# One stacked value product for half of the attention heads, their denominators on VectorE, and key blocks of two head groups in turn

## The chip, the core and the metric

The kernel runs on one core of a Trainium2 chip. The metric is the device time of one execution in microseconds (us).

## What is computed

One encoder layer over 2048 tokens of width 1024. The normalised input goes through one projection whose columns feed two head groups: a gated linear attention (GLA, 4 heads) and a softmax attention with 8 query heads on 2 key/value heads (kv = 0 and 1, four query heads each, head width 64). Both outputs are concatenated, projected, and added to the input; then a mixture of 64 experts follows (each token uses two), and a last norm. The part that changes is the softmax attention:

```
def attend(qb):
    s = jnp.einsum('bkgqd,bksd->bkgqs', qb, kh).astype(jnp.float32)
    p = jax.nn.softmax(s, axis=-1).astype(vh.dtype)
    return jnp.einsum('bkgqs,bksd->bkgqd', p, vh)
```

## The kernel before

The tokens are 16 tiles of 128. A first stage projects the input and stores q, k and v; a second computes the GLA inside chunks and the row maxima of the scores (`maxpass`); the third, which the change touches, holds attention, the output projection and the routing; the fourth runs the experts. Matmuls use a form of f32 with fewer mantissa bits (F32R), so each f32 operand is split into a high part and the low rest, and products of parts are added.

In the third stage a **group** is a token tile i and a kv, and a **key block** is a group and one of 16 tiles of 128 keys: 512 blocks, in the order of `units` (L826): all 16 blocks of a group, then the next group, tiles from the last to the first. A key block (`key_block`, L1310) computes scores of 128 keys by 4 heads x 128 queries with two matmuls into `ps` (L1328, L1329; the second adds the low parts and the negated row maximum), takes the exponential on ScalarE into `p` (L1332), casts it to its high part `p_h` (L1340; on VectorE for two of 16 key tiles, `HDVE`), subtracts to get the low rest `p_l` on VectorE (L1343), and adds three products to the group's accumulator `pa` in PSUM (L1354 to L1356). V holds per key [low (64), high (64), one, one]: high and ones by p_h, low by p_h, high and ones by p_l. The ones give the softmax denominators in rows 64 and 65 of `pa`.

After a group's last block `normalise` (L933) copies `pa` to SBUF on ScalarE (L938), which frees the accumulator (there are two), turns it with four transposes on TensorE (L943), and on VectorE takes the reciprocal of the denominator and multiplies (L949, L950). After kv = 1 of a tile `project` (L974) norms, projects with 48 matmuls (L1007), adds the residual, norms again, and routes the tile's tokens. `gla_out` (L867) finishes the tile's GLA output. The last tile has steps of its own (`linear_half`, `last_part`, `last_rows`), after which the token lists of the experts are ready and the first expert's rows are gathered. `load_ahead` (L1385), issued with the last product, starts the loads of the first expert weights.

The order of instructions on TensorE, VectorE, ScalarE and GpSimd is fixed when the program is built: `Plan` (L121) lets every step ask for an engine with an estimated duration, the tokens it depends on and buffer slots, and each time issues the step that could start first; among those that could start at once, the one whose due time less its urge is smallest. SLOT is the pace by which the due time of the next scores is set. On the chip each engine executes its list in that order and waits on semaphores. SP issues the loads, q of a group by `load_q` (L771) into two buffers.

Of the kernel before, what the change touches and what calls it, by code (L numbers as in the profile page):

```python
# [16 lines left out]
P = 128  # L17
T = 2048
NT = T // P
# [18 lines left out]
GST = 11  # L38
SLOT = 1.7
PACE = 1.6  # L40
# [21 lines left out]
PACE1 = 1.1  # L62
UE, UH, UL, UV = (1,2,3,1)
LPA = 0.2
# [132 lines left out]
def hybrid_encoder_kernel(ctx, tc, x, norm1_gain, w_in, gla_up_fwd, gla_up_fwd_bias, gla_up_bwd,  # L197
# [392 lines left out]
    with ExitStack() as ph:  # L590
# [80 lines left out]
        def maxpass(i):  # L671

            q1 = sp.tile([P, H, P], F32R, name="q1")
            nc.sync.dma_start(q1.bitcast(F32), d_q1[i])
            nm = sp.tile([P, H, 2], F32, name="nm")
            for h in range(H):
                for b in range(2):
                    pm = pp.tile([P, 2, 512], F32, name="pm", bufs=2)
                    for j in range(2):
                        c0 = (2 * b + j) * 512  # L680
                        nc.tensor.matmul(pm[:, j], lhsT=q1[:, h, :], rhs=K1[:, h // 4, c0:c0 + 512],  # L681
                                         start=True, stop=True)
                    nc.vector.tensor_reduce(nm[:, h, b:b + 1], pm, axis=AX.XY, op=OP.max, negate=True)  # L683
                    yield
            nr = sp.tile([P, H], F32R, name="nr")
            nc.vector.tensor_reduce(nr, nm, axis=AX.X, op=OP.min)
            pt = bank("pt")
            nc.tensor.transpose(pt[0:H, 0:P], nr.bitcast(F32), ident)
            nT = sp.tile([H, P], F32, name="nT")
            nc.scalar.copy(nT, pt[0:H, 0:P])  # L690
            nc.sync.dma_start(d_q2[i, DH:DH + 1].rearrange("o h t -> (o h) t"), nT)
            yield
# [87 lines left out]
        for i in range(NT):  # L780
# [3 lines left out]
            if i + 1 < NT:  # L784
                load_u(i + 1)
                decay(i + 1)
            else:

                right.close()
                kvp = right.enter_context(tc.tile_pool(name="pkv", bufs=1, side="right", reuse_waits="tile"))  # L790
                K2 = kvp.tile([DH + 1, NKV, T], F32R, name="K2")
                V = kvp.tile([P, NT, NKV, VW], F32R, name="V")
                nc.sync.dma_start(K2.bitcast(F32), d_K2)
                nc.sync.dma_start(V.bitcast(F32), d_V)
                qp = right.enter_context(tc.tile_pool(name="pcq", bufs=2, side="right", reuse_waits="tile"))
                for kv in range(NKV):
                    load_q(NT - 1, kv)
            g, m = gla(i), maxpass(NT - 1 - i)
# [11 lines left out]
    with ExitStack() as ph:  # L810
# [14 lines left out]
        order = list(reversed(range(NT)))  # L825
        units = [(i, kv, kt) for i in order for kv in range(NKV) for kt in range(NT)]  # L826
        NU, last = len(units), order[-1]
        plan = Plan({"ps": 3, "p_h": NPH, "p_l": NPL, "p": NPP, "acc": 2, "den": 2, "pt": 2, "pm": 1, "mTg": 1, "mTa": 1, "xT": 1,
                     "h": 1, "gla": 1, "route": 1, "on": 1, "oa": 1, "w": 0, "mtg": 0})
        add, give = plan.add, plan.give  # L830
        mTs, ons, acc_o = {}, {}, {}
        prev = [None, None, None, None]
# [7 lines left out]
        def rsqrt_steps(dst, ss, n, t0):  # L840

            w = ss.shape[-1]
            hx = sp.tile([P, w], F32, name=f"hx{w}", bufs=4)
            t = sp.tile([P, w], F32, name=f"nt{w}", bufs=4)
            v = nc.vector
# [87 lines left out]
        def normalise(i, kv, tv):  # L933
# [3 lines left out]
            oa = sp.tile([P, 512], F32, name="oa", bufs=1)  # L937
            nc.scalar.copy(oa[0:DH + 2], pa)  # L938
            give(t, "acc")
            t = yield ask("pe", 0.45, t, take=("on", "pt") if kv == 0 else ("pt",))  # L940
            pt = pp.tile([P, 4, P], F32, name="pt", bufs=2)
            for h in range(4):
                nc.tensor.transpose(pt[:, h, 0:DH + 2], oa[0:DH + 2, h * P:(h + 1) * P], ident[0:DH + 2, 0:DH + 2])  # L943
            give(t, "oa")
# [343 lines left out]
        def list_columns(i, o12, at, vals, *t):  # L1288
# [19 lines left out]
            return t  # L1308

        def key_block(u):  # L1310

# [4 lines left out]
            if u + 1 < NU:  # L1316
                if kt == NT - 1 and u + NT + 1 < NU:
                    load_q(*units[u + NT + 1][:2])
                    Q[units[u + NT + 1][:2]] += (landed(ts),)
                if kv == 0 and kt == GST:  # L1320
# [12 lines left out]
            give(t, "ps")  # L1333
            hd = kt in HDVE or (u < HN and kt in HD0)
            if hd:
# [7 lines left out]
            nc.vector.tensor_tensor(p_l, p, p_h.bitcast(F32), op=OP.subtract)  # L1343
            give(tl, "p")

            tv = yield ask("pe", 0.7, tl, take=(("acc", f"v{u}") if kt == 0 else (f"v{u}",)), urge=UV)
            if kt == 0:
                acc_o[i, kv] = pp.tile([P, 512], F32, name="pa", bufs=2)[0:DH + 2]
            plan.slots.pop(f"v{u}")
            plan.slots[f"v{u + 1}"] = [(0.0, "pe")]  # L1350

            pa = acc_o[i, kv]
            hi = V[:, kt, kv, DH:2 * DH + 2]
            nc.tensor.matmul(pa, lhsT=hi, rhs=p_h, start=(kt == 0), stop=False)  # L1354
            nc.tensor.matmul(pa[0:DH], lhsT=V[:, kt, kv, 0:DH], rhs=p_h, start=False, stop=False)  # L1355
            nc.tensor.matmul(pa, lhsT=hi, rhs=p_l, start=False, stop=(kt == NT - 1))  # L1356
            give(tv, "p_l", "p_h")
# [368 lines left out]
```

## Time and profile before

| | |
|---|---|
| median of 3 runs | 2979.42 us (2977.94 to 2983.98) |
| the profiled execution | 2981.33 us, of which its span 2979.4 us |
| TensorE busy | 2812.6 us (94%) |
| VectorE busy | 2225.4 us (75%) |
| ScalarE busy | 1852.0 us (62%) |

The shares are averages over four stages with different limits; the third stage lies between about 771 and 1690 us. A matmul's recorded time is longer than the distance to the next one's start, so TensorE's busy time does not tell how many matmuls could still be placed.

### The profile page before, as it was taken

How to read it: one execution, taken by the hardware profiler on the slowest of the kernel's cores; microseconds unless marked ns; L12 is line 12 of the kernel's file. 1: busy time of each engine (PE TensorE's matmuls, PEld its weight loads, DVE VectorE, ACT ScalarE, POOL GpSimd, SP SyncE). 2: the span in 40 equal slices, each digit the busy share in tenths (PEclk: the TensorE clock that was granted, in tenths of full speed). 3: DMA queues.
4: the chain of work that ended last, by engine and by line, in shares of the span. 5: the costliest groups of instructions: out<-in, count | busy, mean ns of one | idle time of the engine just before them, and what ended most of it. 6: DMA issues, size and time to landing. Idle time of an engine off the chain costs nothing.

```text
span 2979.4 us, 38648 instructions
## 1 busy us (share of the span) xinstructions
PE 2812.6 (94%) x13776; PEld 2101.0 (71%) x13776; DVE 2225.4 (75%) x3222; ACT 1852.0 (62%) x2776; POOL 448.4 (15%) x326
## 2 busy tenths in 40 slices
PE   7999899999999999999999799999999999999992
PEld 6888688887677777777776566676676666666771
DVE  6655688888676677776666788888788878778783
ACT  4433333333677777777776567777777777777773
POOL 3433111111000000000000121111111112122111
PEclk9999999999899999999999899999999999999996
DMA  7884422233521121121221799999999999999986
GB/s 254 283 279 162 149 105 91 94 105 118 198 66 63 63 80 59 61 80 58 66 77 42 249 371 365 358 355 353 352 364 353 354 353 357 350 345 357 353 311 236
DMA packets 175140, 647.00 MB, mean 217 GB/s; under 512 B 38885, under 2 KB 53575, under 8 KB 119325
## 3 DMA queue, kind: packets, MB, share of 16 engines
q1 hardware_dynamic: 136766, 590.92, 54.3%
q0 software_dynamic: 23712, 34.36, 5.3%
q10 hardware_dynamic: 14464, 19.21, 2.0%
q8 instruction: 109, 1.79, 0.2%
q14 instruction: 89, 0.73, 0.1%
HBM read 546.08 MB, written 117.13 MB: 223 GB/s over the span
## 4 chain that ended last, share of the span: by engine, by line
PE 59%; DMA 21%; issue 7%; DVE 6%; ACT 5%; POOL 1%; ACTq 0%; SPq 0%; POOLq 0%; DVEq 0%
DMA raw<-in_w_gate_dram 10%; DMA raw<-in_w_up_dram 7%; PE pm L1007 6%; PE pm L681 4%; PE pa L1356 4%; PE ps L1328 4%; PE pa L1354 4%; PE pa L1355 4%; PE py L1575 4%; PE pg L1569 4%; PE ps L1329 4%; PE pv L334 3%; PE pqk L334 3%; DVE wl L1505 2%; ACT wh L1503 2%
## 5 line engine op out<-in xcount | busy, mean ns | idle before, releaser
L1505 DVE TENSOR_TENSOR wl<-raw,wh 128x2048 fp32r<-128x2048 f32 x384 | 873.5, 2289 | 218.2 <-ACT wh L1503 215.6
L1503 ACT CAST wh<-raw 128x2048 fp32r<-128x2048 f32 x384 | 727.0, 1908 | 272.5 <-DMA raw<-in_w_up_dram 146.9
L1343 DVE TENSOR_TENSOR p_l<-p,p_h 128x512 fp32r<-128x512 f32 x512 | 343.8, 689 | 199.4 <-ACT p_h L1340 193.1
L1332 ACT ACTIVATE p<-ps 128x512 f32<-128x512 f32 x512 | 296.4, 599 | 150.0 <-PE ps L1329 129.4
L683 DVE TENSOR_REDUCE nm<-pm 128x1 f32<-128x1024 f32 x256 | 304.9, 1216 | 46.7 <-PE pm L681 46.5
L1569 PE MATMUL pg<-wh,xT 128*100 128x512 f32 x1024 | 335.4, 398 | 0.0
L1569 PE MATMUL pu<-wh,xT 128*100 128x512 f32 x1024 | 330.7, 394 | 0.0
L1575 PE MATMUL py<-wh,hT 128*100 128x512 f32 x1024 | 320.7, 416 | 0.0
L1340 ACT CAST p_h<-p 128x512 fp32r<-128x512 f32 x448 | 269.0, 624 | 5.8
L1514 POOL DMA_INDIRECT xg<-d_xn,L x64 | 109.2, 1707 | 914.6 <-PE pt L1540 904.5
L1569 PEld LDWEIGHTS pu<-wh,xT 128*100 128x100 f32 x1024 | 168.1, 164 | 68.2
L1569 PEld LDWEIGHTS pg<-wh,xT 128*100 128x100 f32 x1024 | 170.7, 167 | 64.6
L1328 PE MATMUL ps<-q,K 128*128 128x512 f32 x512 | 210.6, 411 | 1.2 <-ACT p L1332 0.8
L1575 PEld LDWEIGHTS py<-wh,hT 128*100 128x100 f32 x1024 | 170.3, 176 | 55.6
L1354 PE MATMUL pa<-p_h,V 128*66 128x512 f32 x512 | 204.3, 399 | 0.0
L1356 PE MATMUL pa<-p_l,V 128*66 128x512 f32 x512 | 202.6, 396 | 0.9 <-DVE p_l L1343 0.9
L1329 PE MATMUL ps<-q,K 65*128 65x512 f32 x512 | 203.2, 397 | 0.0
L1569 PE MATMUL pg<-wl,xT 128*100 128x512 f32 x512 | 202.0, 395 | 0.0
L1355 PE MATMUL pa<-p_h,V 128*64 128x512 f32 x512 | 201.4, 393 | 0.0
L1569 PE MATMUL pu<-wl,xT 128*100 128x512 f32 x512 | 200.5, 392 | 0.0
L681 PE MATMUL pm<-K,q 128*128 128x512 f32 x512 | 169.6, 416 | 1.1 <-DVE nm L683 1.1
L1575 PE MATMUL py<-wl,hT 128*100 128x512 f32 x512 | 166.3, 407 | 0.0
(415 smaller groups left out, 5041.9 us busy)
## 6 DMA issues: line engine op xcount, KB each, us to landing
raw<-in_w_gate_dram SPq DMA_DIRECT2D x128, 1024.0 KB
raw<-in_w_up_dram SPq DMA_DIRECT2D x128, 1024.0 KB
raw<-in_w_down_dram SPq DMA_DIRECT2D x128, 1024.0 KB
d_uT<-uT SPq DMA_DIRECT2D x16, 1024.0 KB
uT<-d_uT SPq DMA_DIRECT2D x15, 1024.0 KB
x_t<-in_x_dram SPq DMA_DIRECT2D x16, 512.0 KB
wraw<-in_w_in_dram SPq DMA_DIRECT2D x32, 256.0 KB
d_q<-q ACTq DMA_DIRECT2D x16, 512.0 KB
```

What stands on the lines that cost most here:

```text
L683: nc.vector.tensor_reduce(nm[:, h, b:b + 1], pm, axis=AX.XY, op=OP.max, negate=True)
L1328: nc.tensor.matmul(ps, lhsT=K1[:, kv, ks], rhs=r1, start=True, stop=False)
L1329: nc.tensor.matmul(ps, lhsT=K2[:, kv, ks], rhs=r2, start=False, stop=True)
L1332: nc.scalar.activation(p, ps, AF.Exp)
L1343: nc.vector.tensor_tensor(p_l, p, p_h.bitcast(F32), op=OP.subtract)
L1354: nc.tensor.matmul(pa, lhsT=hi, rhs=p_h, start=(kt == 0), stop=False)
L1355: nc.tensor.matmul(pa[0:DH], lhsT=V[:, kt, kv, 0:DH], rhs=p_h, start=False, stop=False)
L1356: nc.tensor.matmul(pa, lhsT=hi, rhs=p_l, start=False, stop=(kt == NT - 1))
L1503: nc.scalar.copy(wh, raw)
L1505: lo = nc.vector.tensor_tensor(wl, raw, wh.bitcast(F32), op=OP.subtract)
L1569: nc.tensor.matmul(acc_p, lhsT=xTs[e][:, a, k, :], rhs=w[:, kk, :], start=(k == 0 and a == 0 and w is wh), stop=(k == KD - 1 and a == 1))
L1575: nc.tensor.matmul(acc_p[:, c], lhsT=hTs[e][:, a, k, :], rhs=w[:, kk, c * 512:(c + 1) * 512], start=(k == 0 and a == 0 and w is wh), stop= ...
```

## The change

Blocks of kv = 0 use one product with V's [low, high] as 128 weight columns and p_h, which puts low x p_h in rows 0 to 63 of `pa` and high x p_h in rows 64 to 127, and a second with high and p_l, added to rows 0 to 63. The ones are no longer in it: the denominators' partial sums are kept per key partition in a tile `den` on VectorE (`denominators`: a copy for the first block of a group, an addition for the fifteen others), and p is released when both subtraction and addition are done. `normalise` for kv = 0 turns and adds both halves at once with four f32 products against two stacked identities (`two`, written over a mask that is no longer used), and sums `den` over the partitions with four f32 products against ones. Blocks of kv = 1 are as before. The casts of kv = 0 are all on ScalarE. The order of the blocks alternates between the second half of one group and the first half of the next, so that a kv = 0 and a kv = 1 block take turns. There are three q buffers, loaded ahead for three groups, and some small tiles have fewer buffers. SLOT goes from 1.7 to 1.6.

```
-SLOT = 1.7
+SLOT = 1.6
...
-UE, UH, UL, UV = (1,2,3,1)
+UE, UH, UL, UV, US = (1,2,3,1,1.5)
...
-            nT = sp.tile([H, P], F32, name="nT")
+            nT = sp.tile([H, P], F32, name="nT", bufs=1)
...
-                qp = right.enter_context(tc.tile_pool(name="pcq", bufs=2, side="right", reuse_waits="tile"))
-                for kv in range(NKV):
-                    load_q(NT - 1, kv)
+                qp = right.enter_context(tc.tile_pool(name="pcq", bufs=3, side="right", reuse_waits="tile"))
+                for n in range(3):
+                    load_q(NT - 1 - n // NKV, n % NKV)
...
-        units = [(i, kv, kt) for i in order for kv in range(NKV) for kt in range(NT)]
+        groups = [(i, kv) for i in order for kv in range(NKV)]
+        half = lambda g, a: [groups[g] + (kt,) for kt in range(a * NT // 2, (a + 1) * NT // 2)] if 0 <= g < len(groups) else []
+        units = []
+        for g in range(len(groups) + 1):
+            old, new = half(g - 1, 1), half(g, 0)
+            units += [u for pair in zip(old, new) for u in pair] if old and new else old + new
+        two = cs["mf"][:, 0:DH]
+        nc.vector.tensor_tensor(two, ident[:, 0:DH], ident[:, DH:P], op=OP.add)
...
-            hx = sp.tile([P, w], F32, name=f"hx{w}", bufs=4)
-            t = sp.tile([P, w], F32, name=f"nt{w}", bufs=4)
+            hx = sp.tile([P, w], F32, name=f"hx{w}", bufs=3)
+            t = sp.tile([P, w], F32, name=f"nt{w}", bufs=3)
...
-            nc.scalar.copy(oa[0:DH + 2], pa)
+            nc.scalar.copy(oa if kv == 0 else oa[0:DH + 2], pa)
             give(t, "acc")
-            t = yield ask("pe", 0.45, t, take=("on", "pt") if kv == 0 else ("pt",))
+            t = yield ask("pe", 0.45 if kv else 0.9, t, take=("on", "pt", f"sum{i}") if kv == 0 else ("pt",))
             pt = pp.tile([P, 4, P], F32, name="pt", bufs=2)
             for h in range(4):
-                nc.tensor.transpose(pt[:, h, 0:DH + 2], oa[0:DH + 2, h * P:(h + 1) * P], ident[0:DH + 2, 0:DH + 2])
+                hs = slice(h * P, (h + 1) * P)
+                if kv:
+                    nc.tensor.transpose(pt[:, h, 0:DH + 2], oa[0:DH + 2, hs], ident[0:DH + 2, 0:DH + 2])
+                else:
+                    nc.tensor.matmul(pt[:, h, 0:DH], lhsT=oa[:, hs], rhs=two, start=True, stop=True)
+                    nc.tensor.matmul(pt[:, h, DH:DH + 2], lhsT=dens[i][:, hs], rhs=cs["one"][:, 0:2], start=True, stop=True)
...
+        def denominators(i, kt, t, p, done):
+            t = yield ask("dve", 0.69 if kt else 0.44, t, take=(f"sum{i}",) if kt else ("den",), urge=US)
+            if kt == 0:
+                dens[i] = sp.tile([P, 512], F32, name="den")
+                nc.vector.tensor_copy(dens[i], p)
+            else:
+                nc.vector.tensor_tensor(dens[i], dens[i], p, op=OP.add)
+            give(t, f"sum{i}")
+            done.append(t)
+            if len(done) == 2:
+                give(t, "p")
...
-                if kt == NT - 1 and u + NT + 1 < NU:
-                    load_q(*units[u + NT + 1][:2])
-                    Q[units[u + NT + 1][:2]] += (landed(ts),)
+                if kt == NT - 1 and len(Q) < len(groups):
+                    nxt = groups[len(Q)]
+                    load_q(*nxt)
+                    Q[nxt] += (landed(ts),)
...
-            hd = kt in HDVE or (u < HN and kt in HD0)
+            done = []
+            if kv == 0:
+                add(denominators(i, kt, t, p, done))
+            hd = kv and kt in HDVE
...
-            hi = V[:, kt, kv, DH:2 * DH + 2]
-            nc.tensor.matmul(pa, lhsT=hi, rhs=p_h, start=(kt == 0), stop=False)
-            nc.tensor.matmul(pa[0:DH], lhsT=V[:, kt, kv, 0:DH], rhs=p_h, start=False, stop=False)
-            nc.tensor.matmul(pa, lhsT=hi, rhs=p_l, start=False, stop=(kt == NT - 1))
+            if kv == 0:
+                for part in ("hl", "lh")[kt == NT - 1]:
+                    if part == "h":
+                        nc.tensor.matmul(pa, lhsT=V[:, kt, kv, 0:2 * DH], rhs=p_h, start=(kt == 0), stop=(kt == NT - 1))
+                    else:
+                        nc.tensor.matmul(pa[0:DH], lhsT=V[:, kt, kv, DH:2 * DH], rhs=p_l, start=False, stop=False)
+            else:
+                hi = V[:, kt, kv, DH:2 * DH + 2]
+                nc.tensor.matmul(pa, lhsT=hi, rhs=p_h, start=(kt == 0), stop=False)
+                nc.tensor.matmul(pa[0:DH], lhsT=V[:, kt, kv, 0:DH], rhs=p_h, start=False, stop=False)
+                nc.tensor.matmul(pa, lhsT=hi, rhs=p_l, start=False, stop=(kt == NT - 1))
```

## Rows read from the trace of the kernel before

**Rows 1.** The page's head and busy times: busy us (share) xinstructions.
```profile
span 2979.4 us, 38648 instructions
...
PE 2812.6 (94%) x13776; PEld 2101.0 (71%) x13776; DVE 2225.4 (75%) x3222; ACT 1852.0 (62%) x2776; POOL 448.4 (15%) x326
...
PEclk9999999999899999999999899999999999999996
```
**Rows 2.** Busy time by stretch; columns in the first line.
```profile
core 0: us, PE busy (x) PEld busy (x) DVE busy (x) ACT busy (x) POOL busy (x), PEclk, DMA share, GB/s
771.00:811.00 40.00, 39.68 (x178) 26.73 (x177) 25.80 (x51) 33.56 (x71) 0.00 (x0) 0.97 0.79 281
...
871.00:1591.00 720.00, 716.93 (x3598) 515.77 (x3597) 506.46 (x1319) 535.92 (x1184) 26.36 (x26) 1.00 0.22 68
...
1651.00:1691.00 40.00, 21.04 (x114) 16.61 (x113) 28.35 (x92) 17.24 (x32) 10.42 (x9) 0.71 0.57 217
...
1700.00:2970.00 1270.00, 1167.18 (x5327) 847.10 (x5325) 1007.87 (x664) 895.27 (x724) 228.02 (x132) 0.96 0.97 347
```
**Rows 3.** Groups by line, 871 to 1591 us: busy us, mean ns, idle before.
```profile
L1343 DVE TENSOR_TENSOR p_l<-p,p_h 128x512 fp32r<-128x512 f32 x416 | 279.6, 688 | 155.3 <-ACT p_h L1340 150.7 <-issue 0.3
L1332 ACT ACTIVATE p<-ps 128x512 f32<-128x512 f32 x415 | 240.7, 599 | 120.2 <-PE ps L1329 101.2 <-DVE pr L1254 8.1 <-DVE p_l L1343 5.0
L1340 ACT CAST p_h<-p 128x512 fp32r<-128x512 f32 x364 | 218.6, 624 | 4.9
L1328 PE MATMUL ps<-q,K 128*128 128x512 f32 x415 | 170.2, 410 | 0.9 <-ACT p L1332 0.4
L1354 PE MATMUL pa<-p_h,V 128*66 128x512 f32 x414 | 165.2, 399 | 0.0
L1356 PE MATMUL pa<-p_l,V 128*66 128x512 f32 x415 | 164.3, 396 | 0.7 <-DVE p_l L1343 0.7
```
**Rows 4.** Timeline of TensorE around a group's end: start us, us, what.
```profile
1031.26 0.40 PE L1328 MATMUL ps<-q,K 128*128 128x512 f32 x1
...
1032.66 0.39 PE L1356 MATMUL pa<-p_l,V 128*66 128x512 f32 x1
...
1035.45 0.40 PE L1329 MATMUL ps<-q,K 65*128 65x512 f32 x1
...
1037.00 0.41 PE L943 MATMUL pt<-cst_sb,oa 66*128 66x66 f32 x4
```
**Rows 5.** Timeline of TensorE's weight loads at 965 us: the rank products.
```profile
965.02 0.42 PEld L1248 LDWEIGHTS pt<-ohb,cst_sb 128*128 128x128 f32 x2
965.37 0.30 PEld L1249 LDWEIGHTS pt<-acc,cst_sb 128*128 128x128 f32 x2
965.59 0.19 PEld L1328 LDWEIGHTS ps<-q,K 128*128 128x128 f32 x1
```
**Rows 6.** VectorE: timeline near 778 us, and the rows of tile den.
```profile
777.84 0.43 DVE L1340 CAST p_h<-p 128x512 fp32r<-128x512 f32 x1 [0.21 <-ACT p L1332]
778.35 1.90 DVE L1343 TENSOR_TENSOR p_l<-p,p_h 128x512 fp32r<-128x512 f32 x3
...
L1157 DVE TENSOR_TENSOR den<-p,g x2: 682/684/685, 1660.5 to 1662.4; 128x512 f32<-128x512 f32 x2
```
**Rows 7.** Timeline of ScalarE around the same group's end.
```profile
1035.56 0.59 ACT L938 COPY oa<-pa 66x512 f32<-66x512 f32 x1
```
**Rows 8.** The chain that ended last, from the last products on.
```profile
1649.20 0.24 PE pa L1354
1649.89 0.89 PE pt L1074 x12
...
1653.11 0.78 PE pt L1074 x12
...
1678.32 5.49 DMA xg<-d_xn,L
...
1686.47 19.98 DMA raw<-in_w_down_dram
```

More of the change, by code (lines that the diff above doesn't have):

```diff
@@ L830, in hybrid_encoder_kernel @@
         add, give = plan.add, plan.give
-        mTs, ons, acc_o = {}, {}, {}
+        mTs, ons, acc_o, dens = {}, {}, {}, {}
         prev = [None, None, None, None]
@@ L937, in normalise @@
             oa = sp.tile([P, 512], F32, name="oa", bufs=1)
-            nc.scalar.copy(oa[0:DH + 2], pa)
+            nc.scalar.copy(oa if kv == 0 else oa[0:DH + 2], pa)
             give(t, "acc")
-            t = yield ask("pe", 0.45, t, take=("on", "pt") if kv == 0 else ("pt",))
+            t = yield ask("pe", 0.45 if kv else 0.9, t, take=("on", "pt", f"sum{i}") if kv == 0 else ("pt",))
             pt = pp.tile([P, 4, P], F32, name="pt", bufs=2)
             for h in range(4):
-                nc.tensor.transpose(pt[:, h, 0:DH + 2], oa[0:DH + 2, h * P:(h + 1) * P], ident[0:DH + 2, 0:DH + 2])
+                hs = slice(h * P, (h + 1) * P)
[5 more added lines that the diff above has]
+            if kv == 0:
+                give(t, "den")
             give(t, "oa")
@@ L1343, in key_block @@
             nc.vector.tensor_tensor(p_l, p, p_h.bitcast(F32), op=OP.subtract)
-            give(tl, "p")
-            tv = yield ask("pe", 0.7, tl, take=(("acc", f"v{u}") if kt == 0 else (f"v{u}",)), urge=UV)
+            done.append(tl)
+            if kv or len(done) == 2:
+                give(tl, "p")
+            tv = yield ask("pe", 0.7 if kv else 0.47, tl, take=(("acc", f"v{u}") if kt == 0 else (f"v{u}",)), urge=UV)
             if kt == 0:
-                acc_o[i, kv] = pp.tile([P, 512], F32, name="pa", bufs=2)[0:DH + 2]
+                acc_o[i, kv] = pp.tile([P, 512], F32, name="pa", bufs=2)[0:DH + 2 if kv else P]
             plan.slots.pop(f"v{u}")
@@ L1352, in key_block @@
             pa = acc_o[i, kv]
-            hi = V[:, kt, kv, DH:2 * DH + 2]
-            nc.tensor.matmul(pa, lhsT=hi, rhs=p_h, start=(kt == 0), stop=False)
-            nc.tensor.matmul(pa[0:DH], lhsT=V[:, kt, kv, 0:DH], rhs=p_h, start=False, stop=False)
-            nc.tensor.matmul(pa, lhsT=hi, rhs=p_l, start=False, stop=(kt == NT - 1))
+            if kv == 0:
+                for part in ("hl", "lh")[kt == NT - 1]:
[8 more added lines that the diff above has]
+                nc.tensor.matmul(pa, lhsT=hi, rhs=p_l, start=False, stop=(kt == NT - 1))
             give(tv, "p_l", "p_h")
```

## Prediction

> **What bounds the kernel now.** I read the page's head and busy shares first, then the busy times by stretch, then the instruction groups inside the attention stretch, then single rows of TensorE, VectorE and ScalarE, and last the chain that ended last.
>
> The head gives a span of 2979.4 us and TensorE busy 94% of it [rows 1]. A busy TensorE may hide slack, because a matmul is recorded as 0.40 us while its successor starts sooner, so what counts is the distance between starts. The stretches show three regimes [rows 2]. From 771 to 1651 us attention runs. In its steady part, 871 to 1591 us, there are 416 key blocks [rows 3], which is 13 token tiles of 32 blocks, so a tile takes 720/13 = 55.4 us. TensorE is busy in 716.9 of those 720 us at full granted clock, VectorE in 506.5 and ScalarE in 535.9. Per tile that is VectorE 39.0 us and ScalarE 41.2 us of 55.4. From 1651 to 1691 us comes a tail in which every engine waits on a serial chain, and from 1700 us on the experts run with the DMA engines 97% busy.
>
> Is TensorE packed in the steady part? From the score matmul that starts at 1031.26 to the one at 1035.45 there are 18 steps, so 4.19/18 = 0.233 us each [rows 4]. The score and product rows wait under 1 us in all 720 us, while VectorE idles 155.3 us in front of its subtraction and ScalarE 120.2 us in front of its exponential, both waiting for work [rows 3]. So TensorE sets the pace and the two others follow it. That is the reading on which everything rests: 0.233 us taken from TensorE is worth 0.233 us, until another engine runs out of idle time.
>
> What follows attention starts relative to its end. The first expert weights are loaded when the last product is issued, and the token lists are ready at 1678.3 us after the serial chain [rows 8]. So a shorter attention moves the experts forward by as much.
>
> **The change, part by part.**
>
> *One product less.* For kv = 0, 16 tiles x 16 blocks = 256 blocks issue two 512-column matmuls instead of three. The two that stay have the same 512 columns. The wider weights (128 columns, not 66) load in 0.19 us, as the score weights do [rows 5], and that lies beside a 0.233 us matmul. 256 x 0.233 = **-59.6 us**, or 3.73 a tile.
>
> *The turn in normalise becomes ordinary f32 products.* Four transposes, 0.06 us apart and 0.41 us with the last one's tail [rows 4], which occupy about 0.25 us, are replaced once a tile by eight f32 matmuls. The trace shows what an f32 matmul with 128 x 128 weights and 64 columns costs, in the rank products: each is issued twice, and the weight loads starting at 965.37 (two) and the next at 965.59 are 0.11 us apart [rows 5]. Eight products, sixteen loads: 16 x 0.11 = 1.78 us. Less 0.25, that is 1.53 a tile, 16 x 1.53 = **+24.5 us**. The four two-column products have no like in the trace. If their weights set the time, they cost the same; if every step cost only the transposes' 0.06, the sixteen would take 0.98 us and this term would be 11.7. I take the weights' price, the nearest row in shape, and keep 11.7 and 26 as ends. The plan puts 0.9 us on this step, so TensorE falls behind it by 0.9 us a tile; the engines execute a fixed order, so this shifts the others and leaves no hole on TensorE.
>
> *The denominators move to VectorE.* Per tile one copy and fifteen additions of 128 x 512 f32. The like addition took 0.68 us and the cast 0.43 [rows 6]. Three subtractions in a row took 1.90 us, so they started 0.60 apart [rows 6]: 15 x 0.60 to 15 x 0.69, plus 0.43, less two casts of kv = 0 that go to ScalarE (0.87). VectorE's demand is then 47.5 to 48.9 us a tile. TensorE's new tile is 55.4 - 3.73 + 1.53 = 53.2 us. So VectorE is at 89 to 92% and is covered by TensorE, with 4.3 to 5.7 us of idle left where it had 16.4, 11.9 of them in front of the subtraction (155.3/13). ScalarE gets two casts of 0.62: 42.5 of 53.2. In a fixed order VectorE cannot use all idle time: an instruction that waits for its cast holds up the additions behind it, then the products wait, and TensorE with them. I put 0.4 us a tile on this, **+6 us**, between 0 and 1.3 a tile (20 us).
>
> *p is held longer* (subtraction and addition). Exponential, cast and subtraction take 0.60 + 0.62 + 0.69 = 1.9 us; four buffers at 53.2/32 = 1.66 us a block give 6.6. Nothing, unless VectorE is late by over 4 us.
>
> *The alternation.* It pairs a light block (TensorE 0.93, VectorE 1.2 by spacing) with a heavy one (1.17, 0.6). Between two groups' hand-overs it changes no amount of work. At the start, though, eight blocks of kv = 0 run alone: VectorE needs 1.2 us a block, as long as the old block took on TensorE, so their saving of 8 x 0.233 is lost: **+2 us**. At the end eight blocks of kv = 1 run alone at the old price. The project of the last tile but one starts some 24 blocks before the end, not 32; its logits stood at 1649.9 to 1653.9 us already, after the last product at 1649.2 [rows 8], so its routing may push the list chain: **+3 us**, 0 to 6.
>
> *Accumulators.* A group's first product now follows the other group's last by two blocks, while both accumulators are held. The copy that frees one waited in one place from the last product's start at 1032.66 to 1035.56, then took 0.59 [rows 4, 7], 3.5 us; two blocks are 3.3. TensorE has projection steps to place between. 0; the bad end is a rival.
>
> *Loads.* One q pair more is issued on SP ahead of the stage (two DMAs), before the last GLA tile's stores, which block 11 reads first; afterwards one a group as before. The small scratch tiles with a buffer less and the 64-column addition for the stacked identity are used once a tile or once at all. SLOT at 1.6 orders work and makes no engine wait. Together 0.
>
> **Sum.** -59.6 + 24.5 + 6 + 2 + 3 = **-24 us**. The profiled execution took 2981.3 us (its span and 1.9 us around it), so 2957; the median of the three runs is 1.9 us lower, which gives **2955 us**.
>
> **Rivals.**
>
> *VectorE sets part of the pace.* The trace lets VectorE's neighbours overlap by 0.09 us; if the added work comes mostly behind waits, it costs full durations, 48.9 us a tile, and the idle time in front of subtractions must fall from 11.9 to 4.3. If it stays at 5.5, a tile takes 54.4, 1.2 over TensorE's 53.2: 16 x 1.2 = 19 us, 13 beyond the 6 already counted: **2968 us**. For it speaks the fixed order and that 150.7 of the 155.3 us were waits for ScalarE's cast [rows 3]; against it, that VectorE waited because TensorE was slow, so the waits shrink with it. The Trainium skill, "VectorE: DVE Perf Modes", section "The DRAIN you can't avoid", says that the next operation does not start until the pipe is empty; the three subtractions in 1.90 us speak against that here, and if it held, this rival would be the likeliest.
>
> *Accumulator hand-over, the other sign.* If the copy comes as late at every one of 31 hand-overs as the one shown and TensorE has nothing else in order, each costs up to 1.5 us: 31 x 1.5 = 46, giving **3001 us**. It decides from 0.8 us each, where 24 us are eaten. Against it: TensorE keeps other work in the stage, and in the place shown the copy was late only because ScalarE had exponentials in front of it.
>
> *TensorE saves more.* If the sixteen small steps cost 0.06 and no wait is added, -59.6 + 11.7 + 2 = -46: **2933 us**. The weight row speaks against it.
>
> *Nothing comes of it*: the end is set by the DMA-bound experts whatever attention does. Their stream begins with attention's end, which speaks against it: **2979 us**.
>
> **How the numbers follow.** A difference of 0.2% (6 us) is about what a measurement can tell from none. The forecast's own range, its terms at half their bounds, is 2944 to 2965: chance 0.52. VectorE rival 0.22, hand-over 0.08, more saved 0.12, nothing 0.06. Faster by over 0.2% (below 2973.5): 0.52 + 0.12 + most of 0.22 = 0.82. Within: 0.09. Slower: 0.09, the hand-over and what lies beyond VectorE's break-even (6.5 us of idle a tile). The range that leaves out 2 in 10 reaches from 2936, near the saving rival, to 2974.
>
> **What would show it.** In a steady stretch: a tile near 53.5 us; two product rows per kv = 0 block 0.233 us apart; about sixteen small matmuls in 1.8 us for the turn; VectorE near 90% with its added row at 0.69 us mean; idle before the subtraction near 4 us a tile. Wrong would make it: TensorE rows with waits for p_l or for the accumulator's copy that sum to over 10 us; a tail from last product to list longer than 29 us; a granted clock below 1.0 inside the stage.

## The result, and the profile after

The changed kernel takes 2951.35 us, the median of four runs (2948.37 to 2953.23); the kernel before, on the same chip, 2979.55. The ratio is 0.9905, with a 95% interval of 0.9893 to 0.9917: 28 us faster. 2955 was predicted, between 2936 and 2974.

The page of the profiled execution (2948.37 us), its head, busy times and granted clock:

```profile
span 2946.2 us, 38839 instructions
...
PE 2778.5 (94%) x13712; PEld 2099.8 (71%) x13712; DVE 2352.9 (80%) x3447; ACT 1866.2 (63%) x2808; POOL 452.1 (15%) x326
...
PEclk9999999999999999999999799999999999999996
```

The span is 33.2 us shorter than that of [rows 1]. TensorE lost 34.1 us of busy time and kept its share of 94%; VectorE gained 127.5 us. Where the 33.2 us are is read from three moments of both traces: the first score matmul, the first gather of tokens, the end. The first score starts at 765.5 us (771.1 before), the stage from there to the gather lasts 877.3 (907.2), the experts from there to the end 1303.4 (1301.1): 5.6 + 29.9 - 2.3 = 33.2.

The 5.6 us lie ahead of the changed stage. Busy time by stretch, 755 to 772 us, first before, then after; the number behind POOL is the granted clock:

```profile
755.00:772.00 17.00, 13.50 (x41) 9.11 (x40) 10.52 (x15) 2.48 (x5) 1.26 (x1) 0.54 0.12 47
```

```profile
755.00:772.00 17.00, 12.57 (x52) 8.63 (x51) 12.19 (x21) 7.17 (x15) 1.10 (x1) 0.90 0.27 94
```

The clock stood at its lower level (1.2 GHz) for nearly the whole stretch before, for 3.4 us after. Two experiments below (alternation alone with the old SLOT, and the old order without additions) show the long drop as well, others with the same code ahead of the stage a shorter one, so it is nothing that the change did; the medians, 28 us apart, stand near the 29.9 of the stage less 2.3.

Inside the stage, the same steady stretch as in [rows 2]:

```profile
871.00:1591.00 720.00, 718.72 (x3700) 541.32 (x3699) 631.55 (x1566) 563.33 (x1252) 32.39 (x29) 1.00 0.22 69
```

TensorE is still packed (718.7 of 720 us, granted clock 1.00); VectorE went from 506.5 to 631.6, 88%. From block 64 to block 448 a tile takes 53.2 us; it took 55.4. The groups by line of the same 720 us that answer to [rows 3] (busy us, mean ns | idle before, releaser):

```profile
L1376 DVE TENSOR_TENSOR p_l<-p,p_h 128x512 fp32r<-128x512 f32 x426 | 285.3, 687 | 29.5 <-ACT p_h L1373 20.7 <-PE pa L1399 5.0 <-PE pa L1392 0.4
L1362 ACT ACTIVATE p<-ps 128x512 f32<-128x512 f32 x426 | 246.7, 602 | 120.7 <-PE ps L1359 113.1 <-DVE on L966 2.7 <-DVE p_l L1376 1.9
L1358 PE MATMUL ps<-q,K 128*128 128x512 f32 x425 | 172.9, 407 | 1.3 <-ACT p L1362 1.0
L1333 DVE TENSOR_TENSOR den<-den,p 128x512 f32<-128x512 f32 x200 | 137.3, 686 | 18.6 <-ACT p L1362 17.6
L1392 PE MATMUL pa<-p_h,V 128*128 128x512 f32 x214 | 87.6, 410 | 0.0
L1394 PE MATMUL pa<-p_l,V 128*64 128x512 f32 x214 | 84.7, 396 | 0.0
```

L1392 and L1394 are the two products that kv = 0 keeps. VectorE's idle time in front of its subtraction fell from 155.3 to 29.5 us, and 200 additions of 0.69 us came in; ScalarE's in front of its exponential did not move, 120.7 for 120.2, and still waits for scores. The turn of a tile, from TensorE's timeline (start us, us):

```profile
1065.67 0.38 PE L956 MATMUL pt<-cst_sb,oa 128*128 128x64 f32 x2
...
1067.43 0.48 PE L1392 MATMUL pa<-p_h,V 128*128 128x512 f32 x1
```

Eight products, each issued twice, take 1067.43 - 1065.67 = 1.76 us; the mean over the tiles of the stretch is 1.71.

**An account of TensorE.** For every kernel below, TensorE's time from the first score to the first gather is split: the distance from one start to the next counts as *work* up to the median of its own kind (line, tiles and shape), and what is beyond it as *lost*. (The two end with the last matmul's start, 1.6 us ahead of the gather in before and after, so they add up to less than the stage; where a record is missing, its time counts as lost.) *Tile* is the mean from block 64 to block 448. Stage, tile, work and lost are those of one profiled execution of each kernel, and the executions of one kernel lie 1 to 15 us apart, so a few us between two stages are not clear of noise.

```
                                  median us  ratio [95%]               stage  tile   work   lost
before                            2979.55    1                         907.2  55.42  862.0   43.6
after                             2951.35    0.9905 [0.9893, 0.9917]   877.3  53.22  826.8   48.9
e1  after, no additions           2947.91    0.9896 [0.9878, 0.9913]   875.0  53.19  827.0   46.3
e5  after, 4 of 16 added twice    2957.74    0.9928 [0.9911, 0.9946]   885.2  53.60  827.6   56.0
e2  after, old block order        2977.68    0.9987 [0.9976, 0.9998]   904.3  53.87  828.6   74.1
e9  e2, no additions              2971.72    0.9960 [0.9943, 0.9977]   892.8  53.29  827.1   64.1
e11 e9, none in the plan either   2955.46    0.9916 [0.9895, 0.9937]   884.8  53.70  827.0   56.2
e12 e11, 8 casts a tile moved     2953.02    0.9910 [0.9891, 0.9928]   879.4  53.26  829.1   48.7
e3  before, alternating           2990.02    1.0030 [1.0018, 1.0043]   916.5  55.77  860.0   54.9
e8  e3, SLOT 1.7                  2992.42    1.0038 [1.0025, 1.0051]   918.0  55.85  859.8   56.6
e4  after, 64-row transposes      2961.33    0.9940 [0.9920, 0.9961]   892.4  54.13  831.6   59.2
e7  after, another turn           2941.14    0.9864 [0.9845, 0.9883]   867.4  52.93  818.7   47.1
e10 e7, all casts on ScalarE      2940.56    0.9862 [0.9846, 0.9879]   868.4  52.68  821.8   45.0
e6  kv = 1 as well, on GpSimd     3087.10    1.0364 [1.0345, 1.0383]  1012.2  61.58  804.0  206.6
```

Ratios are to the kernel before in the same job. Between before and after, work fell by 35.2 us and lost time rose by 5.3.

### The profile page after: what moved, and what is told of

Same layout as the page of the kernel before. It is cut to its first block, busy times and chain, and to the rows that moved or that the text cites. A ratio compares the mean times of both kernels' runs of the same rounds, so it can differ in the third digit from the quotient of the medians.

```text
span 2946.2 us, 38839 instructions
## 1 busy us (share of the span) xinstructions
PE 2778.5 (94%) x13712; PEld 2099.8 (71%) x13712; DVE 2352.9 (80%) x3447; ACT 1866.2 (63%) x2808; POOL 452.1 (15%) x326
## 4 chain that ended last, share of the span: by engine, by line
PE 60%; DMA 23%; issue 6%; DVE 5%; ACT 4%; POOL 1%; SPq 0%; ACTq 0%; POOLq 0%; DVEq 0%
DMA raw<-in_w_up_dram 11%; DMA raw<-in_w_gate_dram 9%; PE pm L1023 6%; PE pm L681 4%; PE ps L1358 4%; PE pg L1612 4%; PE ps L1359 4%; PE py L1618 3%; PE pv L334 3%; PE pqk L334 3%; DVE wl L1548 3%; PE pg L334 2%; PE pq L334 2%; ACT wh L1546 2%; PE pu L1612 2%
## 5 line engine op out<-in xcount | busy, mean ns | idle before, releaser
L1376 DVE TENSOR_TENSOR p_l<-p,p_h 128x512 fp32r<-128x512 f32 x512 | 342.1, 687 | 35.8 <-ACT p_h L1373 25.5
L1373 ACT CAST p_h<-p 128x512 fp32r<-128x512 f32 x480 | 289.7, 627 | 6.2 <-PE pa L1398 0.6
L1618 PEld LDWEIGHTS py<-wh,hT 128*100 128x100 f32 x1024 | 169.7, 176 | 55.4
L1333 DVE TENSOR_TENSOR den<-den,p 128x512 f32<-128x512 f32 x240 | 164.7, 686 | 21.1 <-ACT p L1362 19.9
L1291 POOL DMA_INDIRECT d_list<-rec_a,di x28 | 31.8, 1134 | 800.7 <-DVE di L1287 381.7
L1660 POOL DMA_INDIRECT d_h<-o,L x64 | 120.2, 1877 | 117.1 <-ACT o L1655 97.8
```

The costliest lines, as they stand in the source:

```text
L1373: (nc.vector.tensor_copy if hd else nc.scalar.copy)(p_h, p)
L1618: nc.tensor.matmul(acc_p[:, c], lhsT=hTs[e][:, a, k, :], rhs=w[:, kk, c * 512:(c + 1) * 512], start=(k == 0 and a == 0 and w is wh), stop= ...
```

## The experiments

**Additions left out (e1).** The instructions and their order stay, except that the denominators' sum is one operation on the first block:

```diff
-                nc.vector.tensor_copy(dens[i], p)
-            else:
-                nc.vector.tensor_tensor(dens[i], dens[i], p, op=OP.add)
+                nc.vector.tensor_scalar(dens[i], p, 16.0, 1.0, op0=OP.mult, op1=OP.add)
```

> Leaves out the fifteen additions of each kv = 0 group: its denominators come from the first block alone, scaled by 16 plus 1. The order of all other instructions is that of the changed kernel. If VectorE is covered by TensorE, a tile stays at 53.2 us (53.0 to 53.3) and the whole within 6 us of the changed kernel. If VectorE sets part of the pace, the tile falls by 0.4 us or more and the whole by 6 to 20 us. VectorE's busy time in 871 to 1591 us falls from 631 to about 500 us in both.

The stage is 2.3 us shorter than in after, the tile 0.03. In the 720 us VectorE falls back to 521.8 us, and its idle time before the subtraction is there again:

```profile
871.00:1591.00 720.00, 718.65 (x3702) 542.21 (x3701) 521.84 (x1365) 563.34 (x1253) 29.11 (x29) 1.00 0.21 69
```

```profile
L1374 DVE TENSOR_TENSOR p_l<-p,p_h 128x512 fp32r<-128x512 f32 x427 | 287.9, 690 | 137.7 <-ACT p_h L1371 118.0 <-PE pa L1397 11.6 <-PE pa L1392 2.6
```

So 110 us of VectorE's work in the 720 cost 2.3 us of stage, and the ratios, 0.9896 and 0.9905 with intervals that overlap, do not tell them from none. TensorE covers them, and the rival in which VectorE sets part of the pace falls.

**More of it (e5).** In every fourth block the sum is added twice, so the denominators come out larger.

```diff
+                for _ in range(2 if kt % 4 == 3 else 1):
+                    nc.vector.tensor_tensor(dens[i], dens[i], p, op=OP.add)
```

> Four of the sixteen blocks of a kv = 0 group execute their addition twice (the denominators come out too large), the planned order is the same. Without any addition the tile took 53.19 us, with fifteen 53.22. VectorE was busy 631.6 of 720 us, 46.7 us a tile; four more additions, each behind the one it depends on, add about 2.9: 49.6 of 53.2. If idle time still covers them, the tile stays under 53.5 us and the whole within 5 us of the changed kernel. If VectorE's fixed order leaves no more room, the tile grows by 0.5 to 2.9 us and the whole by 8 to 45 us.

VectorE, in the same stretch:

```profile
871.00:1591.00 720.00, 716.34 (x3674) 535.67 (x3673) 657.33 (x1601) 562.75 (x1244) 28.57 (x26) 1.00 0.21 69
```

Its waits, TensorE's weight loads from 771 to 1600 us (us in total, times, longest):

```profile
PEld pa L1395 <- DVE p_l L1377: 11.6, 35, 0.8
...
PEld pa L1400 <- DVE p_l L1377: 7.0, 15, 1.3
```

and those of after:

```profile
PEld ps L1358 <- ACT p L1362: 12.6, 34, 0.9
...
PEld pa L1394 <- DVE p_l L1376: 2.7, 9, 0.5
...
PEld pa L1399 <- DVE p_l L1376: 0.8, 3, 0.4
```

At 91% VectorE comes late: 18.6 us of waits for p_l instead of 3.5, 8 us more stage (6 by the medians). The fifteen additions and the copy that the change makes lie just inside the cover.

**The old block order (e2).** All of the change but the alternation. (The turn is planned after the sixteenth addition by name, since in this order the planner could otherwise take it up after any of them.)

```diff
+        units = [(i, kv, kt) for i in order for kv in range(NKV) for kt in range(NT)]
...
-            t = yield ask("pe", 0.45 if kv else 0.9, t, take=("on", "pt", f"sum{i}") if kv == 0 else ("pt",))
+            t = yield ask("pe", 0.45 if kv else 0.9, t, take=("on", "pt", f"all{i}") if kv == 0 else ("pt",))
```

> The changed kernel with the blocks in the old order, 16 of a group and then the next (three q buffers kept; the turn is planned after the sixteenth addition by name). If the alternation only orders work that TensorE has to do anyway, the time is that of the changed kernel within 6 us. If it is what keeps VectorE covered, groups of kv = 0 run at VectorE's pace: a kv = 0 block needs 1.2 us on VectorE beside the tile's other 19 us, so a kv = 0 group of 16 blocks needs about 29 us where its half of a tile's 53.2 is 26.6, and the tile grows by 1 to 2.5 us: 15 to 40 us slower than the changed kernel, which is between 10 us faster and 10 us slower than the kernel before.

Nearly all of the gain is gone, with the same work on TensorE (828.6). It is nearly all waiting; the waits of TensorE's weight loads (its matmuls add 6.9 and 8.5 us on the same two, and the products of kv = 1 another 2.8 for p_l):

```profile
PEld ps L1355 <- ACT p L1359: 29.1, 67, 1.4
PEld pa L1391 <- DVE p_l L1373: 20.7, 35, 2.2
```

That is 36.0 us for the exponential, where after has 15.1, and 32.0 for p_l, where after has 3.5.

Busy time in stretches of 32 us, of e2 and then of after (behind the 32.00 come TensorE, its weight loads, VectorE, ScalarE, GpSimd):

```profile
864.00:896.00 32.00, 27.30 (x114) 17.53 (x112) 29.17 (x60) 26.21 (x55) 0.00 (x0) 0.95 0.15 50
896.00:928.00 32.00, 32.00 (x178) 24.38 (x176) 21.28 (x63) 20.17 (x46) 2.12 (x2) 1.00 0.23 71
928.00:960.00 32.00, 30.88 (x147) 22.61 (x146) 30.82 (x63) 27.46 (x58) 0.00 (x0) 1.00 0.22 71
```

```profile
864.00:896.00 32.00, 32.00 (x168) 24.22 (x167) 25.62 (x56) 24.09 (x56) 0.00 (x0) 1.00 0.24 79
896.00:928.00 32.00, 32.00 (x162) 24.32 (x161) 29.24 (x78) 25.72 (x56) 2.14 (x2) 1.00 0.18 54
928.00:960.00 32.00, 31.79 (x163) 22.93 (x162) 28.78 (x62) 26.84 (x61) 0.00 (x0) 1.00 0.25 79
```

In the old order VectorE's load swings between 21.3 and 30.8 us in these three stretches, and where it is high TensorE has holes; in after it stays between 25.6 and 29.2 and TensorE is full. Over all 25 stretches of 32 us from 800 to 1600 us it lies between 19.7 and 30.8 in e2 and between 25.6 and 30.5 in after. (The granted clock of 0.95 in e2's first row is one fall of 3.4 us, behind a wait.) Over the 720 us VectorE's load is about the same, 616.0 and 631.6. Alternating is worth 27.0 us of stage (904.3 - 877.3), and the next three kernels ask what it consists of.

**The old order without additions (e9), with none in the plan either (e11), and with casts moved (e12).** e9 is e2 with e1's edit: the order of instructions stays that of e2. In e11 the planner is told that an addition takes no time, so it writes a new order. e12 also gives eight of the sixteen casts of kv = 0 to VectorE, which takes load from ScalarE. All three leave the additions out. (The first hunk is e11's and e12's, the second e12's alone.)

```diff
-            t = yield ask("dve", 0.69 if kt else 0.44, t, take=(f"sum{i}",) if kt else ("den",), urge=US)
+            t = yield ask("dve", 0.0 if kt else 0.44, t, take=(f"sum{i}",) if kt else ("den",), urge=US)
...
-            hd = kv and kt in HDVE
+            hd = kt in HDVE if kv else kt % 2 == 1
```

> The old block order with the stacked product, and the fifteen additions of each kv = 0 group left out (denominators from the first block alone, scaled by 16 plus 1); its planned order is that of the run with the old block order and the additions. That run had TensorE waits for p_l of some 32 us. If the alternation is worth 27 us only because it spreads VectorE's additions, leaving them out gives these back: 2978 - 25 to 30, some 2950 us, and the waits for p_l fall under 5 us. If the order itself matters (accumulators, later projections, how the list is planned), it stays above 2965 us.

> As the old block order without additions, but the order of instructions is planned anew with the additions priced at nothing (denominators again from the first block alone, scaled by 16 plus 1). There the stage took 892.8 us, 15.5 more than the changed kernel's 877.3, with scores waiting 36 us for the exponential and products 18 us for p_l. If the order planned for the additions held the rest, the stage falls to 880 or less. If ScalarE is the second limit of kv = 0 groups that stand alone (an exponential and a cast, some 1.0 us a block by their spacing, beside TensorE's 0.93), the stage stays at 885 to 893 and the scores' waits for the exponential stay above 25 us.

> The same, planned anew without additions, and in kv = 0 groups every second cast on VectorE, which has room for it without the additions. If ScalarE's pace in kv = 0 groups is what is left of the alternation's worth, the stage comes to the changed kernel's 877 us within 5 and the scores' waits for the exponential under 18 us, some 2950 us in all. If it is the order itself (accumulators, when projections can start), it stays above 885 us.

The stage goes 904.3, 892.8, 884.8, 879.4, and after has 877.3. Not executing the additions gives 11.5 us back, not planning for them 8.0, the casts 5.4, and 2.1 are left. e9 came out as its second branch, above 2965 us: the additions are not the whole of it. e11 lies between its branches, and e12 meets the numbers of its first. The waits of the weight loads in e9, then in e11, then in e12:

```profile
PEld ps L1353 <- ACT p L1357: 28.9, 66, 1.4
PEld pa L1389 <- DVE p_l L1371: 12.2, 24, 2.3
```

```profile
PEld ps L1353 <- ACT p L1357: 16.4, 40, 1.1
...
PEld pa L1389 <- DVE p_l L1371: 7.8, 27, 0.6
```

```profile
PEld ps L1353 <- ACT p L1357: 12.4, 41, 0.7
PEld pa L1389 <- DVE p_l L1371: 11.3, 18, 2.6
```

Not executing the additions gives the old order 11.5 us and the alternating one 2.3 (e1). So 9.2 of the 27 us are additions that the alternation covers and the old order does not; with none executed, each in the order planned for them, the old order is still 17.8 us behind e1. There TensorE waits, weight loads and matmuls together, 35.8 us for the exponential, as in e2, while its waits for p_l fell from 32.0 to 17.8. What the new plans gave back is not shown to have one cause: e11 has 20.4 us of waits for the exponential and 8.0 for p_l, e12 13.4 and 16.0, so from e11 to e12 one fell, the other rose, and their sum stayed; the medians of the two are 2.4 us apart, and a new plan moves everything. That ScalarE's exponentials and casts are the other load that the alternation evens out is argued from these waits and not shown.

**Alternation alone (e3, e8).** The kernel before, with the new block order, the three q buffers that it needs, the smaller scratch buffers, and SLOT at 1.6 (e3) or 1.7 (e8).

```diff
-        units = [(i, kv, kt) for i in order for kv in range(NKV) for kt in range(NT)]
...
+        for g in range(len(groups) + 1):
+            old, new = half(g - 1, 1), half(g, 0)
+            units += [u for pair in zip(old, new) for u in pair] if old and new else old + new
```

> The kernel before with the alternating order, three q buffers and SLOT 1.6, and nothing else of the change (three products for both kv, no additions). If the whole gain is the product's, the time is that of the kernel before within 6 us and the tile stays at 55.4 us. If the order itself saves TensorE waits, or the later start of the projections helps the stage, it is 6 to 12 us faster; if the accumulators' hand-over two blocks apart makes TensorE wait, it is over 6 us slower, with waits of the first products for the copy.

> The alternating order alone, as before, with SLOT 1.7 instead of 1.6. With 1.6 it was 10 us slower than the kernel before, with TensorE's scores waiting 25 us for the exponential to free a bank and 1 us for the accumulator's copy. If the pace of the scores, set below what TensorE needs for a tile of three products, is the cause, 1.7 gives the time of the kernel before within 4 us. If the alternation itself is, it stays 6 to 12 us slower.

Alternation alone costs 9 us of stage, lost time and not work, and SLOT has no part in it. It is not the accumulator's hand-over: its copy was waited for twice, 0.7 us by a weight load and 0.3 us by a product (the last two lines), while the weight loads' waits for the exponential rose to 25.4 us from 10.0 before. First before, then e3:

```profile
PEld ps L1328 <- ACT p L1332: 10.0, 28, 0.8
PEld pa L1356 <- DVE p_l L1343: 6.5, 15, 0.7
```

```profile
PEld ps L1334 <- ACT p L1338: 25.4, 71, 0.7
PEld pa L1362 <- DVE p_l L1349: 9.6, 28, 0.7
...
PEld pa L1360 <- ACT oa L943: 0.7, 1, 0.7
```

```profile
PE pa L1360 <- ACT oa L943: 0.3, 1, 0.3
```

Why a block order that changes no work brings these waits stays open. Both kernels also have the third q buffer and the smaller scratch buffers, and no run of the kernel before has these alone.

**The turn with transposes (e4).** The f32 products that add the two halves become transposes of the high half; the low half is left out of the result.

```diff
-                    nc.tensor.matmul(pt[:, h, 0:DH], lhsT=oa[:, hs], rhs=two, start=True, stop=True)
+                    nc.tensor.transpose(pt[:, h, 0:DH], oa[DH:P, hs], ident[DH:P, DH:P])
```

> Leaves the low product's half out of the kv = 0 result: the four f32 products with the stacked identity become four transposes of the high half (64 rows), the four products for the denominators stay, and the planned order is the same. The f32 products start 0.11 us apart, two for each (0.88 us a tile); transposes 0.06 apart take 0.25. If each small step on TensorE counts in full, the tile falls by 0.63 us to 52.6 and the whole by 10 us. If the turn is hidden by something else, nothing changes (under 3 us).

Ten us slower where ten faster was expected. One turn and what follows it, on TensorE, and the busy times of the stretch behind it, with the granted clock:

```profile
1069.15 0.27 PE L956 MATMUL pt<-cst_sb,oa 64*128 64x64 f32 x1
1069.35 0.38 PE L957 MATMUL pt<-cst_sb,den 128*128 128x2 f32 x2
...
1071.14 0.48 PE L1392 MATMUL pa<-p_h,V 128*128 128x512 f32 x1
...
1073.16 0.63 PE L1023 MATMUL pm<-woh,mTg 128*128 128x512 f32 x1
1073.59 0.63 PE L1023 MATMUL pm<-wol,mTg 128*128 128x512 f32 x1
```

```profile
1070.00:1078.00 8.00, 8.00 (x31) 6.06 (x32) 4.20 (x14) 3.22 (x7) 0.00 (x0) 0.79 0.08 33
```

A transpose between f32 products takes 0.20 us to the next start (1069.15 to 1069.35), and the turn 1.99 us, longer than the 1.71 of the turn that it replaces; sixteen times 0.28 us are 4.5 of the 4.8 us by which work rose. And in the rows from 1073.16 us on 512-column matmuls start 0.43 apart, not 0.233: the granted clock went to its lower level for 3.4 us, at half of full speed, which makes 0.79 of the 8 us shown. It did so six times between 771 and 1600 us, each 2.0 to 3.4 us after the start of a turn, with no idle time of TensorE between, and never there in after. Six times 3.4 us in which a step takes 0.43 and not 0.233 lose 9.4 us, nearly the rise in lost time (10.3). Work and lost time make the stage 15.1 us longer; the medians are 10.0 apart.

**Another turn (e7, e10).** The denominators' four f32 products first and by themselves; then four transposes of all 128 rows, and the halves are added on VectorE. e10 also puts the two casts a tile that VectorE had for kv = 1 on ScalarE (HDVE = ()).

```diff
-                    nc.tensor.matmul(pt[:, h, 0:DH], lhsT=oa[:, hs], rhs=two, start=True, stop=True)
...
+                nc.tensor.transpose(pt[:, h, 0:n], oa[0:n, h * P:(h + 1) * P], ident[0:n, 0:n])
...
+                nc.vector.tensor_copy(dst, pt[:, :, 0:DH])
+                nc.vector.tensor_tensor(dst, pt[:, :, DH:P], dst, op=OP.add)
```

> The changed kernel with another turn for kv = 0: four products for the denominators, then four transposes of all 128 rows; the two halves are added on VectorE (two operations of 128 x 256 more a tile). TensorE's steps: 8 x 0.11 + 4 x 0.11 = 1.32 us instead of 1.71, 0.4 a tile; VectorE 0.7 more a tile, which the idle time covers. If the steps of the turn count in full and the granted clock stays at 1.0: 5 to 7 us faster than the changed kernel, tile 52.8. If short steps cost something else (as the transposes of 64 rows did, after which the granted clock fell to 0.5 for 3.4 us six times), the time is that of the changed kernel or up to 15 us slower.

> The version with the turn by transposes of 128 rows (2941 us) with the two remaining VectorE casts of a kv = 1 group on ScalarE. VectorE was busy 643 of 720 us there and loses 0.87 us a tile, ScalarE 562 and gains 1.25. If VectorE at 89% still costs waits, as the four doubled additions showed at 91%, it is 2 to 5 us faster; if not, the same within 3 us; if ScalarE's exponentials come later by it, 3 to 10 us slower.

2941.14 us: faster than both kernels, 10 us below after. The parts of a turn in TensorE's timeline:

```profile
1003.36 0.95 PE L953 MATMUL pt<-cst_sb,den 128*128 128x2 f32 x8
1004.16 0.48 PE L1364 MATMUL ps<-q,K 128*128 128x512 f32 x1
...
1015.45 0.60 PE L963 MATMUL pt<-cst_sb,oa 128*128 128x128 f32 x4
1015.80 0.48 PE L1398 MATMUL pa<-p_h,V 128*128 128x512 f32 x1
```

0.80 + 0.35 = 1.15 us instead of 1.76, and the clock stays up. That is more than the 5 to 7 us expected, and it is not the turn alone: of the 9.9 us of stage 3.6 lie between block 64 and block 448, 0.29 us a tile, and 6.7 behind the last score, where the new plan also came out otherwise: the last product starts 7.3 us after the last score and not 12.3. The Trainium skill, "Perfetto Trace Analysis", section "Transposes", wants a logical transpose done as a transpose, not as a matmul. e7 agrees: its four transposes take 0.37 us on the mean, where after's four products with the stacked identity take 0.92; e4 shows that it depends on the form and the neighbours. e10 is level with e7, so the casts' place is worth nothing measurable here.

**Both halves of the heads (e6).** kv = 1 gets two products as well, and its additions go to GpSimd, with three p_h buffers and SLOT 1.55.

```diff
+            t = yield ask(("dve", "pool")[kv], (0.69, 1.35)[kv] if kt else (0.44, 1.2)[kv], t,
...
+            eng = (nc.vector, nc.gpsimd)[kv]
```

> Blocks of kv = 1 get the stacked product too; their denominators are added on GpSimd, where a 128 x 512 f32 operation took 1.27 to 1.64 us in the second stage of the kernel before. All casts are on ScalarE, p_h has three buffers instead of five to make room for the sums, SLOT is 1.55. TensorE's work falls by another 59.6 - 24.5 = 35 us, the tile to 51.0 us. GpSimd gets 20 to 26 us a tile of 51. If TensorE keeps setting the pace: 2951 - 35 = 2916 us, tile 51.0 to 51.6. If the slower sums hold p, or the fewer buffers hold the casts, TensorE waits for p_l or for the exponential: tile 52 to 54, 2930 to 2960 us.

TensorE's work falls by another 22.8 us and the kernel is 107 us slower than before, far outside both branches. Groups by line, and the wait that replaces the work:

```profile
L1333 POOL TENSOR_TENSOR denp<-denp,p 128x512 f32<-128x512 f32 x175 | 264.0, 1509 | 355.4 <-ACT p L1362 353.4 <-issue 0.6
L1375 DVE TENSOR_TENSOR p_l<-p,p_h 128x512 fp32r<-128x512 f32 x375 | 303.7, 826 | 12.2 <-ACT p_h L1372 9.7 <-ACT jb L992 1.5
...
L1333 DVE TENSOR_TENSOR den<-den,p 128x512 f32<-128x512 f32 x176 | 150.5, 855 | 6.5 <-ACT p L1362 6.2
```

```profile
PEld pa L1392 <- DVE p_l L1375: 169.1, 206, 2.7
```

In this kernel VectorE's two-input operations take 826 and 855 ns on the mean instead of 687 and 686. The timelines of GpSimd and VectorE show how:

```profile
813.79 1.41 POOL L1333 TENSOR_TENSOR denp<-denp,p 128x512 f32<-128x512 f32 x1 [2.01 <-ACT p L1362]
```

```profile
813.99 1.77 DVE L1375 TENSOR_TENSOR p_l<-p,p_h 128x512 fp32r<-128x512 f32 x1
```

The subtraction began beside the addition and ended 0.55 us after it. From 871 to 1591 us 302 of VectorE's subtractions and additions met no GpSimd instruction, and none of these took over 0.694 us. Of 244 that did, 101 took longer, up to 2.2 us, and every one of the 101 ended 0.54 to 0.56 us after the end of a GpSimd instruction. What the 244 took beyond the usual 0.683 us adds up to 85 us of the 720, and VectorE is busy in 683 of them. The Trainium skill, "SBUF — State Buffer", section "SBUF: two separate sides", says that a VectorE operation with two inputs in SBUF and a GpSimd one that reads SBUF lock each other out for a whole instruction; these ends agree.

## Why the prediction came out, point by point

*TensorE sets the pace, and the products and the turn are its work.* Shown, though the reading behind it was a little too good: "under 1 us" of waits is that of the matmul rows [rows 3], and the weight loads of the kernel before waited another 10.0 us for the exponential and 6.5 us for p_l (shown under e3). -59.6 + 24.5 = -35.1 was predicted for them, -35.2 measured as work. The turn is 1.71 us a tile (1.78 predicted), the tile 53.2 (53.2).

*Waits by VectorE in the steady part, +6.* The term of the sum that was most mis-sized. From block 64 to 448 lost time went from 24.9 to 24.0 us, so no wait came in; e1 puts the additions' price in the whole stage at 2.3 us, not clear of noise. VectorE needed 631.55/13.53 = 46.7 us a tile of 53.2 (47.5 to 48.9 predicted), and its idle time before the subtraction fell to 29.5/13.53 = 2.2 us, under the 4 that was forecast, and with the 1.4 before additions under the 4.3 on which the rival turned. The rule of the Trainium skill on the empty pipe ("VectorE: DVE Perf Modes", section "The DRAIN you can't avoid"), as the prediction quotes it, would have had neighbours start a full duration apart; the same section adds that a next operation that is not held starts earlier, and VectorE's timeline agrees with that, with starts 0.60 us apart at 0.68 and 0.69 each:

```profile
1040.07 0.69 DVE L1333 TENSOR_TENSOR den<-den,p 128x512 f32<-128x512 f32 x1
1040.67 0.68 DVE L1376 TENSOR_TENSOR p_l<-p,p_h 128x512 fp32r<-128x512 f32 x1
```

*First eight blocks +2, tail +3.* Lost time rose by 3.5 us in the first 64 blocks. From the last score to the gather it was 42.1 us, 37.2 before: +4.9, inside its 0 to 6. The reason given, routing that pushes the list chain, is not shown: 3.9 of the 4.9 us lie between the last score and the last product, and from there to the gather it is 29.8 us, 28.8 before, just past the 29 that the text names as a sign of being wrong. No experiment singles this out.

*Alternation changes no amount of work.* The sentence is true and the price of nothing drawn from it was wrong: 9 us of stage to pay in the old kernel (e3), 27 us of stage to gain in the new one (e2). The sum held because the change contains the alternation; that the saving would nearly go without it stands nowhere in the text, and to that extent the number was luck. The text had a number for part of it: eight blocks of kv = 0 in a row save nothing, since VectorE needs 1.2 us for each. In the old order there are sixteen in a row in every tile, and e2, which has them, has a stage only 2.9 us shorter than that of the kernel before. But e9, which has them without the additions, is still 17.8 us behind e1, so VectorE's load is only part of the reason.

*The rivals.* VectorE's pace: fell by e1, and e5 shows how near it was. Accumulator hand-over: not one of after's waits is for its copy, e3 has 1.0 us. TensorE saves more: its sixteen small steps at 0.06 did not come, the weights' price held (0.112 us from start to start for 64 columns, 0.098 for two). Nothing comes of it: the experts moved forward by what the stage gave.

## What to carry to other kernels

Work moved from the bounding engine to another one can be free in one order and not in another: the same additions cost 2.3 us in the alternating order and 11.5 in the old one. Compare the other engine's demand with the bound over each run of like blocks, not over the whole tile, and when a reorder "changes no work", look whose load it evens out. Test an order with and without the change that it goes with; here it cost 9 us alone and gained 27 beside the stacked product, of which 9 are shown to be the additions. Know how far the cover reaches: at 88% busy the additions cost 2 us at most, at 91% another 8.

## What the runs showed of the hardware

Four transposes of 64 rows, mixed with f32 products, stood 0.20 us each ahead of the next start, where four of 128 rows by themselves took 0.35 us in all. After six of the sixteen turns with such a mixture (e4) the granted clock fell for 3.4 us, about 1.6 us of TensorE's time each, while TensorE showed no idle time. That the turn caused these falls is argued from their place; a turn of e4's form on its own was not run. Falls of 3.4 or 6.8 us also come without it: one each in e2 and e9 and nine in e6, among waits of TensorE, e2's right behind one of 1.74 us.

A VectorE operation with two inputs that ran beside a GpSimd addition often ended only 0.55 us after it, and took up to 2.2 us instead of 0.68 (e6, 101 times in 720 us). VectorE is at 88% in after, came late at 91% in e5, and is at 95% here. e6 also has two p_h buffers less, and how much of its 107 us that is was not tried.
